# Seventeen gate/up pairs of an FFN by Strassen's algorithm, and the sample states moved from the FFN's input to its output stage

## The chip, the cores and the metric

The kernel runs on one core of a Trainium2 chip. The metric is the device time of one execution in microseconds (us). The kernel before took 1107.72 us (median of three runs, 1106.37 to 1108.14).

## The reference

One step of a decoder layer for a prompt of 512 tokens and 8 sample rows, 520 columns in all, with a model width of 1024, all in float32. What the change touches is the end of the layer and one output of its middle:

```
h2 = rmsnorm(x, norm2_w) * (1 + sc2) + sh2
gt, up = jnp.split(h2 @ w_ffn_in, 2, axis=-1)              # 1024 -> 2 x 2816
x = x + g2 * ((jax.nn.silu(gt) * up) @ w_ffn_out)          # 2816 -> 1024
y = rmsnorm(x, final_norm_w)
...
h_last = h0 * decay + B (outer) (x * dt)                   # SSD state of each sample row, ssm_sample
```

The state of each sample row (32 heads x 64 x 128) is read, scaled, increased by an outer product and written out. Nothing else in the layer's end needs it.

## The kernel before, in words

**Number format.** Every matrix product is made of float32 operands that are cut into a high part (ScalarE casts to fp32r) and a low part (VectorE subtracts the high part from the whole). A product is three matmuls: high x high, high x low, low x high. `parts` (lines 110 to 118) cuts a weight block of 128 x 1024, `split` (155 to 157) an activation, `product` (124 to 129) issues the matmuls. All of them stand on line 129 in the profile, all casts of weights on 116, all low parts on 117.

**FFN input stage.** Tokens lie along the free dimension, as two halves of 260. The 22 x 128 gate columns and the 22 x 128 up columns are taken in 22 pairs: `ffn(j)` (L1374) runs `column` for gate block j and for up block j, each 8 blocks of 128 rows x 3 matmuls x 2 halves, so 96 matmuls of 260 columns to a pair. `ffn_end` (L1348) takes silu of the gate on ScalarE (L1354), multiplies it with the up product on VectorE (L1355), and splits the result into `ah` and `al` (L156, L157).

**FFN output stage.** `ffn_out(j)` (L1410) runs one column of 22 blocks x 3 x 2 = 132 matmuls against `ah` and `al`, for j = 0 to 5; its weights come in three pieces of 8, 8 and 6 blocks. VectorE adds the gated product to the residual (`gate_add`), ScalarE squares it (L390), VectorE sums the squares into `acc`. `last_pair` (L1449) runs the last two columns in two token parts and the last norm with them: TensorE sums `acc` over the partitions (L330) in the middle of the second part.

**Sample states.** 32 units, one or two after each pair of the input stage (`sample_state`, L1334). GpSimd makes three elementwise operations for each (L1342 to L1344), and its queue issues the loads of the state (L1330) and of a B row (L1331), and the write (L1345). State loads run two units ahead over three buffers.

**What sets the order.** The program is a list of steps (`todo`); `perform` runs through it and asks `ahead` to load and cut the weights of the next `LOOK` = 2 units before a step is written down. Weight loads go through SP's queue into `raw` tiles, of which there are `NRAW` = 3. TensorE always runs in the order of the program text. The other engines are ordered by a scheduler with priorities. Each engine takes its instructions in order, and an instruction that waits holds those behind it.

Of the kernel before, what the change touches and what calls it, by code (L numbers as in the profile page):

```python
# [16 lines left out]
P = 128  # L17
T = 520
# [34 lines left out]
def tile_decoder(ctx: ExitStack, tc: tile.TileContext, I: dict, O: dict):  # L53
# [129 lines left out]
    def perform():  # L183
        queue = W["queue"] = [u for us, _ in plan for u in us]
        made = W["made"]
        at = 0
        for us, fn in plan:
            ahead(at + len(us) + (LOOK if at else 0), W["loads"] if made else 0)
# [1035 lines left out]
    def out_open():  # L1224
        for n in ("gt_", "gh_", "tb_"):
            closed(G[n])
        closed(G["ab_"])
        closed(G["yp_"])
        G["fp_"], fp = opened("fp")
        x1 = G["x1"] = fp.tile([P, KD, T], F32, name="x1")  # L1230
        G["RB"] = fp.tile([P, T], F32, name="RB3")
# [7 lines left out]
        G["wo_"], G["wo"] = opened("wo")  # L1239
        a2 = mod[:, U_SC2 : U_SC2 + 8]  # L1240
# [68 lines left out]
    def ffn_act():  # L1309
        closed(G["wo_"])  # L1310
        closed(G["mp_"])
        G["hs_"], G["hs"] = opened("hs")
        G["fq_"], fq = opened("fq", "right")
        G["ah"] = fq.tile([P, NF, T], F32R, name="ah")
        G["al"] = fq.tile([P, NF, T], F32R, name="al")

# [6 lines left out]
    def state_load(n):  # L1323
# [9 lines left out]

    def sample_state(n):  # L1334

        g, b = state_unit(n)
        for i in range(0 if n else 2):
            state_load(i)
        h, bb = states.pop(n)
        at = lambda v: v[:, 2 * g : 2 * g + 2, b : b + 2].rearrange("p j b -> p b j").unsqueeze(3).broadcast_to([P, 2, 2, P])  # L1340
        t = G["hs"].tile([P, 2, 2, P], F32, tag="ht", name=f"ht{n}")
        nc.gpsimd.tensor_tensor(t, bb.unsqueeze(2).broadcast_to([P, 2, 2, P]), at(xds), ALU.mult)  # L1342
        nc.gpsimd.tensor_tensor(h, h, at(dtx[:, 1]), ALU.mult)
        nc.gpsimd.tensor_tensor(h, h, t, ALU.add)  # L1344
        nc.gpsimd.dma_start(out=O["ssms"][g, :, b : b + 2], in_=h)  # L1345
        state_load(n + 2)

    def ffn_end(j, pg, pu):  # L1348

        s = G["ff"].tile([P, T], F32, tag="fs", name=f"fs{j}", bufs=NFS)  # L1350
        with urgent():
            for (g, t0, t1), (u, _, _) in zip(pg, pu):
                view = halves if t1 - t0 == T else lambda ap: ap
                nc.scalar.activation(view(s[:, t0:t1]), g, AF.Silu, bias=0.0, scale=1.0)  # L1354
                nc.vector.tensor_tensor(view(s[:, t0:t1]), u, view(s[:, t0:t1]), ALU.mult)  # L1355
        split(G["ah"][:, j], G["al"][:, j], s)

# [50 lines left out]
    ah, al = (lambda k: G["ah"][:, k]), (lambda k: G["al"][:, k])

    def ffn_out(j):  # L1410
        def fn(*ws):
            ps = column(ws, ah, al)
            x = G["x1"][:, j]
# [35 lines left out]
    def last_pair(*ws):  # L1449
# [139 lines left out]
```

## Time and profile before

| | |
|---|---|
| time, median of 3 runs | 1107.72 us |
| the profiled execution | 1108.36 us |
| its span (first to last instruction) | 1106.6 us |
| TensorE, VectorE, ScalarE, GpSimd busy | 1076.7, 695.7, 463.9, 345.5 us |
| first multiply of pair 0, last of pair 21 (L1355) | 721.1 and 963.8 us |
| first matmul of the output stage | 963.5 us |
| last matmuls of the last pair (L129) | about 1092 us |

Times inside the execution count from the start of its span. A row of a group reads: line, engine, operation, what it writes <- what it reads, shapes, how often; then busy us, mean ns of one; then the engine's idle time just before them and what ended it. A row of a timeline reads: start, duration, engine, line, operation. In a row of windows, behind the stretch and its length, stand busy us and count of TensorE, its weight loads, VectorE, ScalarE and GpSimd, then TensorE's granted clock, the share of the DMA engines and GB/s. A row of a DMA view ends in KB of one transfer and the median us from its issue to its landing; a row of one line or tile gives the shortest, median and longest duration in ns. A row of waits reads: who waited <- for what, us in total, times, longest.

### The profile page before, as it was taken

The page shows a single profiled execution, that of the slowest core. Times are in us where ns is not written, and L with a number is a line of the kernel's source. Part 1 is how long each engine was busy: PE and PEld are TensorE (multiplying, and loading weights), DVE is VectorE, ACT ScalarE, POOL GpSimd, SP SyncE. Part 2 cuts the span into 40 slices and gives each one's busy share as a digit, 9 for nine tenths or more (in the row PEclk, how much of TensorE's full clock was granted, in tenths as well). Part 3 has the DMA queues.
Part 4 walks back from the last instruction along what each step waited for, and adds up shares of the span by engine and source line. Part 5 has one row for each costly group of instructions (what it writes and reads, how often), then busy time and mean ns, then how long its engine had stood idle before and what let it go on. Part 6 is the DMA issues. An engine that isn't in the chain of part 4 may idle for free.

```text
span 1106.6 us, 22150 instructions
## 1 busy us (share of the span) xinstructions
PE 1076.7 (97%) x9331; PEld 1047.9 (95%) x9331; DVE 695.7 (63%) x963; ACT 463.9 (42%) x774; POOL 345.5 (31%) x498
## 2 busy tenths in 40 slices
PE   8988999999999999999999999999999999999995
PEld 6987999999999999999999999799999999999995
DVE  5696787877877698688677655556555543323332
ACT  4448464664664534755433333632222222222220
POOL 1133344243333442000000000489999950000001
PEclk8999999999999999999999999999999999999998
DMA  9435453534624423454434445277666642232212
GB/s 360 193 88 173 144 151 122 191 108 132 191 97 135 170 94 126 135 171 153 153 134 159 147 169 189 91 226 218 202 217 197 208 154 96 86 91 88 86 53 78
DMA packets 58467, 165.34 MB, mean 149 GB/s; under 512 B 10880, under 2 KB 16512, under 8 KB 57600
## 3 DMA queue, kind: packets, MB, share of 16 engines
q1 hardware_dynamic: 51712, 142.96, 39.5%
q0 software_dynamic: 6656, 20.98, 6.3%
q8 instruction: 73, 1.20, 0.4%
q14 instruction: 26, 0.21, 0.1%
HBM read 151.05 MB, written 12.86 MB: 148 GB/s over the span
## 4 chain that ended last, share of the span: by engine, by line
PE 86%; DVE 4%; DMA 3%; ACT 2%; issue 2%; POOL 1%; SPq 0%; DVEq 0%; ACTq 0%; POOLq 0%
PE m L129 75%; PE b L129 4%; DMA raw<-in_win 2%; PE b L795 1%; PE b L207 1%; PE b L770 1%; PE b L797 1%; PE b L301 1%; DVE v L652 1%; PE b L748 1%; POOL hst L775 0%; PE b L731 0%; DVE acc L391 0%; DVE wlo L117 0%; DMA araw<-in_wada 0%
## 5 line engine op out<-in xcount | busy, mean ns | idle before, releaser
L129 PE MATMUL m<-hh,whi 128*128 128x260 f32 (+1 forms) x1840 | 380.8, 287 | 4.5 <-ACT v L644 3.4
L129 PE MATMUL m<-hl,whi 128*128 128x260 f32 (+1 forms) x1840 | 374.4, 284 | 1.1 <-DVE hl L481 1.0
L129 PE MATMUL m<-hh,wlo 128*128 128x260 f32 (+1 forms) x1840 | 374.4, 284 | 0.1
L117 DVE TENSOR_TENSOR wlo<-raw,whi 128x1024 fp32r<-128x1024 f32 (+2 forms) x169 | 231.6, 1373 | 162.6 <-ACT whi L116 159.5
L116 ACT CAST whi<-raw 128x1024 fp32r<-128x1024 f32 (+2 forms) x169 | 173.1, 1027 | 356.2 <-PE m L129 240.5
L129 PEld LDWEIGHTS m<-hh,whi 128*128 128x128 f32 x1840 | 286.0, 189 | 10.4 <-ACT v L644 3.6
L129 PEld LDWEIGHTS m<-hl,whi 128*128 128x128 f32 x1840 | 285.5, 189 | 2.0 <-DVE hl L481 1.6
L129 PEld LDWEIGHTS m<-hh,wlo 128*128 128x128 f32 x1840 | 286.0, 189 | 0.3 <-DVE wlo L117 0.3
L341 POOL TENSOR_TENSOR r<-me,mhalf 128x5 f32<-128x5 f32 (+2 forms) x6 | 6.4, 1064 | 438.2 <-DVE me L340 438.2
L652 DVE SCALAR_TENSOR_TENSOR v<-xb,cwh,v 128x512 f32<-128x512 f32 x96 | 72.1, 752 | 39.9 <-POOL xb L639 19.1
L129 PE MATMUL m<-ah,whi 128*128 128x260 f32 x264 | 53.2, 283 | 0.0
L129 PE MATMUL m<-ah,wlo 128*128 128x260 f32 x264 | 53.1, 282 | 0.0
L129 PE MATMUL m<-al,whi 128*128 128x260 f32 x264 | 53.0, 282 | 0.0
L129 PE MATMUL m<-gh,whi 128*128 128x260 f32 x256 | 52.8, 288 | 0.0
L643 ACT COPY xb<-m 128x520 f32<-128x520 f32 (+1 forms) x31 | 17.9, 577 | 82.2 <-PE m L129 82.2
L1355 DVE TENSOR_TENSOR fs<-m,fs 128x520 f32<-128x520 f32 (+2 forms) x23 | 15.5, 676 | 57.4 <-PE m L129 56.6
L129 PE MATMUL m<-gl,whi 128*128 128x260 f32 x256 | 51.3, 282 | 0.0
L129 PE MATMUL m<-gh,wlo 128*128 128x260 f32 x256 | 51.3, 282 | 0.0
L816 POOL TENSOR_TENSOR h<-h,cc 128x1024 f32<-128x1024 f32 x16 | 39.1, 2444 | 27.4 <-DMA cc<-dbc 26.4
L1342 POOL TENSOR_TENSOR ht<-bb,xds 128x512 f32<-128x512 f32 x32 | 45.3, 1415 | 2.4 <-DMA bb<-dbc 1.9
L1344 POOL TENSOR_TENSOR hs<-hs,ht 128x512 f32<-128x512 f32 x32 | 45.2, 1411 | 0.8
L129 PEld LDWEIGHTS m<-gh,whi 128*128 128x128 f32 x256 | 39.2, 188 | 2.6 <-PE b L301 1.3
(300 smaller groups left out, 1742.6 us busy)
## 6 DMA issues: line engine op xcount, KB each, us to landing
raw<-in_win SPq DMA_DIRECT2D x73, 512.0 KB, 4.9
raw<-in_wfi SPq DMA_DIRECT2D x44, 512.0 KB, 4.4
araw<-in_wada SPq DMA_DIRECT2D x24, 512.0 KB, 3.9
h<-in_sssm SPq DMA_DIRECT2D x16, 512.0 KB, 4.0
raw<-in_wssd SPq DMA_DIRECT2D x16, 512.0 KB, 3.4
hs<-in_sssm POOLq DMA_DIRECT2D x32, 256.0 KB, 4.1
out_ssms<-hs POOLq DMA_DIRECT2D x32, 256.0 KB, 3.3
raw<-in_wfo SPq DMA_DIRECT2D x16, 512.0 KB, 3.5
```

What stands on the lines that cost most here:

```text
L116: nc.scalar.copy(hi, raw)
L117: nc.vector.tensor_tensor(lo, raw, hi.bitcast(F32), ALU.subtract)
L129: nc.tensor.matmul(o, a[:, k, c0 : c0 + P], b[:, t0:t1], start=f, stop=e)
L207: nc.tensor.matmul(ps[32 * i : 32 * i + 32, 0:n], sc[:, k], raw[:, n * i : n * i + n], start=first, stop=last)
L301: nc.tensor.matmul(ps[32 * i : 32 * i + 32, 0:256], scr[:, k], w[:, 256 * i : 256 * i + 256], start=k == 0 and j == 0, stop=k == KD - 1 an ...
L643: nc.scalar.copy(shape(xb[:, 3 + t0 : 3 + t1]), o)
L652: nc.vector.scalar_tensor_tensor(v[:, 0:TP], xb[:, k : k + TP], w(k), v[:, 0:TP], ALU.mult, ALU.add)
L748: nc.tensor.matmul(cb[:, cs], bt[:, cs], ct[:, cs], start=True, stop=True)
L816: nc.gpsimd.tensor_tensor(h0, h0, cc.unsqueeze(2).broadcast_to([P, 4, 2, P]), ALU.mult)
L1342: nc.gpsimd.tensor_tensor(t, bb.unsqueeze(2).broadcast_to([P, 2, 2, P]), at(xds), ALU.mult)
L1344: nc.gpsimd.tensor_tensor(h, h, t, ALU.add)
L1355: nc.vector.tensor_tensor(view(s[:, t0:t1]), u, view(s[:, t0:t1]), ALU.mult)
```

## The change

**Seven products for eight.** Pairs 3 to 19 (`WINO = 3, 20`) are computed by the Winograd form of Strassen's algorithm. The gate block and the up block of a pair are taken as a 2 x 2 block matrix (upper and lower half of the 1024 rows by gate and up), the activations as another (upper and lower half of the rows by the two token halves). `wino` runs seven products of 4 blocks x 3 matmuls, each into a single PSUM bank, in the order g0, g1, y0, x1, y1, z0, x0, and VectorE adds them up out of PSUM. `sums_of_rows` makes the four sums of activation blocks once, behind pair 1, on VectorE and GpSimd, and splits them into `tt`. For each pair `wino_weights` cuts the gate block (cut g) and the lower half of the up block (cut x0), then `wino_sums` makes four sums of weight blocks on GpSimd, in place in the raw tiles, and cuts them: x1 from the first sum, y0 from the third, z from the fourth, y1 from the second. All of it for pair j + 1 is written down while pair j runs. The raw tiles stay three.

**The order of the engines.** From `ffn_act` to the end of the output stage all five engines run in the order of the program text instead of the scheduler's.

**Splitting later.** `ffn_end` no longer splits. The 22 results stay in `as` tiles; ten are split before each of the pairs 20 and 21 and two at the end (`out_rows`, `out_row`), when the space of the Strassen tiles is free.

**States later.** The 32 state units become a generator that is stepped five times in each of the six output columns, and to its end before the last pair. One of the three GpSimd operations becomes four ScalarE activations of 128 x 128, one becomes a VectorE addition, one stays. Each step adds and writes the state of the step before. State tiles have four buffers instead of three.

```diff
+WINO = 3, 20
...
     def ffn_act():
...
-        G["hs_"], G["hs"] = opened("hs")
+        G["ffn"] = tc.manual_schedule(engines={E.PE, E.Activation, E.DVE, E.Pool, E.SP})
+        G["ffn"].__enter__()
+        W["loads"] = 0
...
     def state_load(n):
...
-        h = sp.tile([P, 2, 2, P], F32, tag="hs", name=f"hs{n}", bufs=3)
+        h = sp.tile([P, 2, 2, P], F32, tag="hs", name=f"hs{n}", bufs=4)
         bb = sp.tile([P, 2, P], F32, tag="bb", name=f"bb{n}", bufs=3)
...
+    def sample_states():
+        for n in range(2):
+            state_load(n)
+        before = None
+        for n in range(33):
+            if n < 32:
+                g, b = state_unit(n)
+                state_load(n + 2)
+                h, bb = states.pop(n)
+                at = dtx[:, 1, 2 * g : 2 * g + 2, b : b + 2].rearrange("p j b -> p b j")
+                nc.gpsimd.tensor_tensor(h, h, at.unsqueeze(3).broadcast_to([P, 2, 2, P]), ALU.mult)
...
+                        nc.scalar.activation(t[:, i, j], bb[:, i], AF.Identity, bias=0.0, scale=x)
+            if before:
+                pg, pb_, ph, pt = before
+                nc.vector.tensor_tensor(ph, ph, pt, ALU.add)
+                nc.gpsimd.dma_start(out=O["ssms"][pg, :, pb_ : pb_ + 2], in_=ph)
+            before = (g, b, h, t)
+            yield True
...
     def ffn_end(j, pg, pu):
...
-        split(G["ah"][:, j], G["al"][:, j], s)
...
+    def sums_of_rows():
...
+        for k in range(4):
...
+            p(t3, b[0][1][1], b[0][0][1], minus)
+            p(t3, t3, b[1][1][1], add)
+            p(t3, t3, b[1][0][1], minus)
+            v(t1, b[0][0][1], b[0][0][0], minus)
...
+            v(t4, t4, b[1][1][0], add)
+            for i, t in enumerate((t1, t2, t4, t3)):
+                split(*(x[:, k] for x in G["tt"][(0, 1, 3, 2)[i]]), t)
...
+    def wino_load(j):
+        if WINO[0] <= j < WINO[1]:
+            WW["raw", j] = load(I["wfi"][j]), load(I["wfi"][NF + j])
...
+    def wino_weights(j):
...
+        nc.scalar.copy(hi, g)
+        nc.vector.tensor_tensor(lo, g, hi.bitcast(F32), ALU.subtract)
+        wino_tiles(j, "x")
+        split(*(t[:, 0:4] for t in WW["x", j]), u[:, 4:8])
...
+    def wino_sums(j, between=lambda: None, silu=lambda: None):
...
+        a11, a12, a21, a22 = g[:, 0:4], g[:, 4:8], u[:, 0:4], u[:, 4:8]
...
+        v = nc.gpsimd.tensor_tensor
+        v(a22, a21, a22, ALU.add)
+        v(a21, a11, a21, ALU.subtract)
+        v(a11, a22, a11, ALU.subtract)
+        v(a12, a12, a11, ALU.subtract)
+        cuts = [("x", 1, a22), ("y", 0, a11), ("z", 0, a12), ("y", 1, a21)]
...
+        for hi, lo, a in cuts[:2]:
+            nc.scalar.copy(hi, a)
+        silu()
+        for hi, lo, a in cuts[:2]:
+            nc.vector.tensor_tensor(lo, a, hi.bitcast(F32), ALU.subtract)
+        between()
+        for hi, lo, a in cuts[2:]:
+            split(hi, lo, a)
+        wino_load(j + 1)
...
+    def wino(j):
...
+            nc.scalar.copy(u2, mult("g", 0, B(0, 0)))
+            add(sa, mult("g", 1, B(1, 0)), u2)
+            wino_weights(j + 1)
+            add(u2, mult("y", 0, tt[1]), u2)
+            add(u4, mult("x", 1, tt[0]), u2)
+            o = mult("y", 1, tt[2])
+            add(vb, o, u4)
+            add(va, o, u2)
+            add(sb, mult("z", 0, B(1, 1)), u4)
+            o = mult("x", 0, tt[3])
+            def silu():
+                nc.scalar.activation(s, s, AF.Silu, bias=0.0, scale=1.0)
+            def between():
+                add(va, o, va)
+                nc.vector.tensor_tensor(s, f2, s, ALU.mult)
+            wino_sums(j + 1, between, silu)
...
     def ffn_out(j):
         def fn(*ws):
-            ps = column(ws, ah, al)
+            ps = column(ws, ah, al, lambda kk: states_step() if kk in (4, 8, 12, 16, 20) else None)
```

**VectorE during one pair of the input stage.** Before, pair 10: `fs10` is the multiply, `wlo` the low part of a weight block, `al` the low part of the result.

```order
L1355 TENSOR_TENSOR fs10_10287<-m577_10238,fs10_10287 128x520
L117 TENSOR_TENSOR wlo579_10313<-raw578_10310,whi579_10312 128x1024
L157 TENSOR_TENSOR al_8963<-fs10_10287,ah_8962 128x520
L117 TENSOR_TENSOR wlo581_10319<-raw580_10316,whi581_10318 128x1024
L1355 TENSOR_TENSOR fs11_10420<-m583_10371,fs11_10420 128x520
```

Now, from the second product of pair 7 on: `wglo8`, `wxxlo8`, `wyylo8`, `wzlo8` are low parts of the cuts g, x, y, z of pair 8; `raw564` holds its gate block, `raw565` its up block; `b...` are PSUM banks of pair 7's products, `fs7_0`, `fs7_1` and `as7` its sums.

```order
L1496 TENSOR_TENSOR wglo8_9935<-raw564_9900,wghi8_9934 128x1024
L158 TENSOR_TENSOR wxxlo8_9939<-raw565_9902,wxxhi8_9938 128x512
L1545 TENSOR_TENSOR fs7_0_9904<-b568_9942,fs7_0_9904 128x260
L1545 TENSOR_TENSOR fs7_0_9904<-b569_9956,fs7_0_9904 128x260
L1545 TENSOR_TENSOR fs7_1_9905<-b570_9970,fs7_0_9904 128x260 x2
L1545 TENSOR_TENSOR as7_8982<-b571_9985,fs7_0_9904 128x260
L1521 TENSOR_TENSOR wxxlo8_9939<-raw565_9902,wxxhi8_9938 128x512
L1521 TENSOR_TENSOR wyylo8_10013<-raw564_9900,wyyhi8_10012 128x512
L1545 TENSOR_TENSOR fs7_1_9905<-b572_9999,fs7_1_9905 128x260
L1562 TENSOR_TENSOR as7_8982<-fs7_1_9905,as7_8982 128x520
L158 TENSOR_TENSOR wzlo8_10015<-raw564_9900,wzhi8_10014 128x512
L158 TENSOR_TENSOR wyylo8_10013<-raw565_9902,wyyhi8_10012 128x512
```

The two whole-block subtractions and the two results of a pair became one whole block and five half blocks, and seven adds out of PSUM stand among them. The last reader of `raw564` is the low part of z, last but one in the row; the load of pair 9's up block goes into that tile.

**GpSimd around one sample state.** Before, in the input stage: `hs` are state tiles, `bb` B rows, `ht` the outer product.

```order
L1342 TENSOR_TENSOR ht5_9654<-bb5_9527,xds_94 128x512
L1343 TENSOR_TENSOR hs5_9526<-hs5_9526,dtx_93 128x512
L1331 DMA bb7_9660<-dbc_97 128x256
L1344 TENSOR_TENSOR hs5_9526<-hs5_9526,ht5_9654 128x512
L1343 TENSOR_TENSOR hs6_9650<-hs6_9650,dtx_93 128x512
L1345 DMA out_ssms<-hs5_9526 128x512
L1330 DMA hs7_9659<-in_sssm 128x512
```

Now, in the output stage:

```order
L1363 DMA out_ssms<-hs4_12032 128x512
L1337 DMA hs8_12214<-in_sssm 128x512
L1338 DMA bb8_12215<-dbc_97 128x256
L1353 TENSOR_TENSOR hs6_12104<-hs6_12104,dtx_93 128x512
L1363 DMA out_ssms<-hs5_12068 128x512
L1337 DMA hs9_12250<-in_sssm 128x512
```

Two of the three GpSimd operations left its queue. The load of state 7 went into the tile of state 4 (three buffers); the load of state 8 now goes into the tile of state 4 (four buffers), whose write stands just ahead of it in the queue.

More of the change, by code (lines that the diff above doesn't have):

```diff
@@ L187, in perform @@
         for us, fn in plan:
-            ahead(at + len(us) + (LOOK if at else 0), W["loads"] if made else 0)
+            ahead(at + len(us) + (W["look"] if at else 0), W["loads"] if made else 0)
             got = [made[at + i] for i in range(len(us))]
@@ L1332, in state_load @@
         states[n] = h, bb
[L1334 to L1346, printed above, removed]
@@ new lines, in states_step, with __init__, tile @@
+    def states_step():
+        if "states" not in G:
+            G["states"] = sample_states()
+        return next(G["states"], False)
+    class Scratch:
+        def __init__(self):
+            self.at = {"hi": 0, "lo": 0}
+        def tile(self, shape, dtype, tag=None, name=None, bufs=1):
+            kind = tag.split("_")[0]
+            rows = G["hl" if kind == "lo" else "hh"].rearrange("p a b -> p (a b)")
+            if kind == "sq":
+                return G["ff"].tile([P, T], F32, tag="fs", name=name, bufs=NFS)
+            a = self.at[kind]
+            n = shape[1] * shape[2]
+            self.at[kind] += n
+            return rows[:, a : a + n].rearrange("p (k c) -> p k c", c=shape[2])
@@ L1358, in ffn_first, with out_row, out_rows, fn @@
+    def out_row(k):
+        s, hi = G["as"][k], G["ah"][k]
+        lo = G["fq"].tile([P, T], F32R, tag="as", name=f"al{k}", bufs=NF + 1)
+        G["al"].append(lo)
+        split(hi, lo, s)
+    def out_rows(a, b):
+        def fn():
+            for k in range(a, b):
+                out_row(k)
+        return fn
     def ffn_first(part):
@@ new lines, in wino_sums @@
+    def wino_sums(j, between=lambda: None, silu=lambda: None):
+        if not WINO[0] <= j < WINO[1]:
+            silu()
+            between()
+            return
+        g, u = WW.pop(("raw", j))
+        a11, a12, a21, a22 = g[:, 0:4], g[:, 4:8], u[:, 0:4], u[:, 4:8]
+        wino_tiles(j, "y")
+        wino_tiles(j, "z")
+        v = nc.gpsimd.tensor_tensor
[4 more added lines that the diff above has]
+        cuts = [("x", 1, a22), ("y", 0, a11), ("z", 0, a12), ("y", 1, a21)]
+        cuts = [(*(t[:, 4 * h : 4 * h + 4] for t in WW[n, j]), a) for n, h, a in cuts]
+        for hi, lo, a in cuts[:2]:
+            nc.scalar.copy(hi, a)
+        silu()
+        for hi, lo, a in cuts[:2]:
+            nc.vector.tensor_tensor(lo, a, hi.bitcast(F32), ALU.subtract)
+        between()
+        for hi, lo, a in cuts[2:]:
+            split(hi, lo, a)
+        wino_load(j + 1)
@@ new lines, in wino, with fn, mult @@
+    def wino(j):
+        def fn():
+            f1, f2 = (G["ff"].tile([P, T], F32, tag="fs", name=f"fs{j}_{i}", bufs=NFS) for i in range(2))
+            u2, u4, va, vb = f1[:, 0:H2], f1[:, H2:T], f2[:, 0:H2], f2[:, H2:T]
+            s = G["as"][j]
+            sa, sb = s[:, 0:H2], s[:, H2:T]
+            tt = G["tt"]
+            B = lambda r, c: (hblock("hh", r, c), hblock("hl", r, c))
+            def mult(kind, half, x):
+                hi, lo = WW[kind, j]
+                o = bank()[:, 0:H2]
+                for k in range(4):
+                    q = 4 * half + k
+                    for a, b, f, e in ((hi, x[0], k == 0, False), (hi, x[1], False, False), (lo, x[0], False, k == 3)):
+                        nc.tensor.matmul(o, a[:, q], b[:, k], start=f, stop=e)
+                return o
+            add = lambda out, a, b: nc.vector.tensor_tensor(out, a, b, ALU.add)
+            nc.scalar.copy(u2, mult("g", 0, B(0, 0)))
+            add(sa, mult("g", 1, B(1, 0)), u2)
+            wino_weights(j + 1)
+            add(u2, mult("y", 0, tt[1]), u2)
[11 more added lines that the diff above has]
+            wino_sums(j + 1, between, silu)
+            for kind in "gxyz":
+                WW.pop((kind, j))
```

101 lines of the change are left out of this document (82 added, 19 removed).

## The prediction

> **What bounds the kernel now.** I read the page first, then the stretches by window, then the timeline of the FFN input stage.
>
> ```profile
> span 1106.6 us, 22150 instructions
> PE 1076.7 (97%) x9331; PEld 1047.9 (95%) x9331; DVE 695.7 (63%) x963; ACT 463.9 (42%) x774; POOL 345.5 (31%) x498
> PE 86%; DVE 4%; DMA 3%; ACT 2%; issue 2%; POOL 1%; SPq 0%; DVEq 0%; ACTq 0%; POOLq 0%
> ```
>
> TensorE is busy for 97% of the span and makes 86% of the chain that ended last. The windows say whether that is so in the two stages that change:
>
> ```profile
> 850.00:900.00 50.00, 50.00 (x419) 50.00 (x418) 28.12 (x18) 12.70 (x16) 49.05 (x49) 1.00 0.62 194
> 950.00:1000.00 50.00, 50.00 (x419) 50.00 (x418) 15.51 (x22) 13.24 (x16) 0.00 (x0) 1.00 0.31 94
> ```
>
> In both, 419 matmuls in 50 us at a granted clock of 1.00: 119.3 ns each, no gap. In the first, GpSimd is full too (49.05 of 50, the sample states); VectorE and ScalarE have room. The timeline of VectorE gives the period of one gate/up pair:
>
> ```profile
> 929.19 0.70 DVE L1355 TENSOR_TENSOR fs<-m,fs 128x520 f32<-128x520 f32 x1 [3.72 <-PE m L129]
> 930.02 1.23 DVE L117 TENSOR_TENSOR wlo<-raw,whi 128x1024 fp32r<-128x1024 f32 x1
> 931.16 0.69 DVE L157 TENSOR_TENSOR al<-fs,ah 128x520 fp32r<-128x520 f32 x1
> 940.73 0.70 DVE L1355 TENSOR_TENSOR fs<-m,fs 128x520 f32<-128x520 f32 x1 [3.72 <-PE m L129]
> ```
>
> 940.73 - 929.19 = 11.54 us for 96 matmuls. So TensorE bounds the stage, and only what stays below its pace is free.
>
> **What the products save.** A Strassen pair has 7 products of 4 x 3 matmuls: 84 for 96, each still 260 wide, so 84 x 119.3 = 10.02 us. That is 1.43 us for each of 17 pairs, 24.3 us, if TensorE keeps the pace.
>
> **The loop around a Strassen pair.** What must run in turn, once per pair, is priced from the quiet part of the stage:
>
> ```profile
> L117 DVE TENSOR_TENSOR wlo<-raw,whi 128x1024 fp32r<-128x1024 f32 x10 | 12.2, 1225 | 20.3 <-ACT whi L116 19.6
> L116 ACT CAST whi<-raw 128x1024 fp32r<-128x1024 f32 x10 | 10.5, 1054 | 41.8 <-issue 21.1 <-PE m L129 20.7
> L1355 DVE TENSOR_TENSOR fs<-m,fs 128x520 f32<-128x520 f32 x5 | 3.5, 700 | 18.6 <-PE m L129 18.6
> L157 DVE TENSOR_TENSOR al<-fs,ah 128x520 fp32r<-128x520 f32 x5 | 3.5, 694 | 0.0
> L156 ACT CAST ah<-fs 128x520 fp32r<-128x520 f32 x5 | 3.1, 627 | 0.0
> raw<-in_wfi SPq DMA_DIRECT2D x5, 512.0 KB, 3.5
> 925.50 0.33 SPq L107 DMA_DIRECT2D raw<-in_wfi  x1
> 924.25 1.23 DVE L117 TENSOR_TENSOR wlo<-raw,whi 128x1024 fp32r<-128x1024 f32 x1 [3.93 <-ACT whi L116]
> L1344 POOL TENSOR_TENSOR hs<-hs,ht x32: 1290/1308/2159, 725.2 to 897.6; 128x512 f32<-128x512 f32 x32
> ```
>
> A weight load is issued 0.02 us after VectorE releases its buffer (924.25 + 1.23 = 925.48, then 925.50) and lands 3.5 us later. A 512-wide piece costs a little under the 520-wide rows: 0.62 on ScalarE, 0.68 on VectorE. A GpSimd sum of two 128x512 tiles takes 1.30.
>
> There are three raw buffers and each pair takes two, so the up weights of pair n+1 land in the buffer that held the gate weights of pair n. Their load waits for the last reader there, VectorE's low part of cut z. And z is the fourth of four GpSimd sums in a row, each reading the one before; the first overwrites half of the up weights, so it waits for the load and for cut x0. Hence a ring: load 3.5, cast x0 0.62, low x0 0.68, four sums 5.2, cast z 0.62, low z 0.68, an estimated 0.3 for the handovers (one of them is the 0.02 above): **11.6 us at the least**, longer than TensorE's 10.02 and than the 11.54 of today.
>
> Two things lengthen it. First, VectorE takes its work in order: low y0, the add of product 7 (0.43, by the 0.424 of a 256-wide multiply in the last row below), the multiply of 0.69, then low z. Second, GpSimd and VectorE hinder each other:
>
> ```profile
> 803.88 1.41 POOL L1342 TENSOR_TENSOR ht<-bb,xds 128x512 f32<-128x512 f32 x1
> 804.29 1.55 DVE L157 TENSOR_TENSOR al<-fs,ah 128x520 fp32r<-128x520 f32 x1
> 805.25 1.50 POOL L1343 TENSOR_TENSOR hs<-hs,dtx 128x512 f32<-128x512 f32 x1
> L1343 POOL TENSOR_TENSOR hs<-hs,dtx x32: 1047/1072/2025, 722.6 to 896.5; 128x512 f32<-128x512 f32 x32
> L1355 DVE TENSOR_TENSOR fs<-m,fs x23: 424/700/700, 721.1 to 963.8; 128x520 f32<-128x520 f32 x21, 128x256 f32<-128x256 f32 x1, 128x264 f32<-128x264 f32 x1
> ```
>
> The 0.69 us subtraction lasts 1.55 beside GpSimd: it gets going when L1342 ends at about 805.3, and L1343 (1.07 by median) lasts 1.50 as it waits for the subtraction in turn. The multiply out of PSUM never takes more than 0.70, beside GpSimd or not. In the ring: from the release, landing at 3.5, x0 low at 4.9, two sums at 7.5; low x1 squeezes in, so the third sum ends at 9.35 and the fourth at 10.65; low y0, blocked until then, ends at 11.3; add 11.75, multiply 12.45, low z **13.1**. I take 13.1: it is the case without slack, but every row of it is measured. Ends: 11.6, and 14.1 with the load at 4.5, the median in the busy stretch (row below). The four single PSUM banks add nothing: product 7 waits for the bank of product 3, whose add stands behind low x0, and that wait lies inside the 3 us that TensorE idles anyway.
>
> The Trainium skill says of this port (SBUF — State Buffer, "SBUF: two separate sides") that GpSimd and a VectorE instruction with two SBUF inputs lock each other out for a whole instruction. The rows above agree. Without the lock the ring would be 12.1 and the sum below 16 us smaller.
>
> **The sums of rows, before pair 3.** 44 VectorE instructions 260 wide and 12 on GpSimd stand behind pair 1's multiply; pair 3's cuts stand behind them.
>
> ```profile
> 732.92 0.70 DVE L1355 TENSOR_TENSOR fs<-m,fs 128x520 f32<-128x520 f32 x1 [2.75 <-PE m L129]
> L157 DVE TENSOR_TENSOR hl<-xn,hh 128x256 fp32r<-128x256 f32 x8 | 3.1, 422 | 2.0 <-ACT hh L156 2.0
> L1440 POOL TENSOR_TENSOR x<-x,RB 128x256 f32<-128x256 f32 x2 | 1.4, 736 | 5.5 <-ACT RB L1436 5.5
> ```
>
> 44 x 0.427 = 18.8 us; with GpSimd's 12 x 0.74 locked out, 27.7. I take 24, as GpSimd starts early. From 733.6 that is 757.6; pair 2 hides only 11.5 of it. Then low g, low x0, three sums with low x1 between, the rest of the fourth, low y0: 766.1 for the start of pair 3's third product; low z 766.8. Sixteen rings: 976.4; pair 19's y0 stands 1.8 before, 974.6. Five products (7.16), the add, the multiply and pair 20's first low part (2.35 and 0.2, less the 0.5 that needs only high parts): pair 20 starts at 983.8. Before, it starts two pairs ahead of the output stage:
>
> ```profile
> L129 PE MATMUL m<-ah,whi x264: 278/283/286, 963.5 to 1058.0; 128*128 128x260 f32 x132
> 1078.23 0.50 PE L330 MATMUL b<-cst,acc 128*128 128x1 f32 x4
> ```
>
> 963.5 - 23.1 = 940.4. **Term 1: +43.4 us** (19 with a ring of 11.6, 59 with 14.1; 4 either way for the sums). At TensorE's own pace of 10.02 it is -5.9. The row splits in pairs 20 and 21 cost nothing: ten of 0.69 and two weight parts of 1.23 are 9.4 of VectorE's 11.5 us. The norm row moved to another pool adds no instruction.
>
> **The states in the output stage.** Taking them out of the input stage gains nothing by itself: TensorE had no gap there. Per state and in GpSimd's order: state load, B load, multiply, write of the state before.
>
> ```profile
> raw<-in_wfi SPq DMA_DIRECT2D x31, 512.0 KB, 4.5
> out_ssms<-hs POOLq DMA_DIRECT2D x31, 256.0 KB, 3.2
> out_ssms<-hs POOLq DMA_DIRECT2D x1, 256.0 KB, 2.5
> out_ssms<-hs POOLq DMA_DIRECT2D x1, 256.0 KB, 4.9
> L1331 POOL DMA_DIRECT2D bb<-dbc x32 | 18.7, 585 | 0.0
> L1345 POOL DMA_DIRECT2D out_ssms<-hs x32 | 18.2, 568 | 0.6 <-POOL hs L1344 0.6
> L1330 POOL DMA_DIRECT2D hs<-in_sssm x32 | 18.0, 561 | 1.4 <-DMA out_ssms<-hs 0.9 <-issue 0.6
> POOL hs L1330 <- DMA out_ssms<-hs: 0.9, 1, 0.9
> ```
>
> With four buffers, load n+2 takes the buffer of state n-2, and that one is written out as the last thing of the step before. So GpSimd issues a write and then stands at the next load until it has landed. Before, the load waited for an older write: 0.9 us in the whole stage. One step is now 3.2 + 0.56 + 0.59 + 1.07 + 0.1 = **5.5 us**; 4.8 with the quickest write shown, 7.2 with the slowest; five steps, 27.5, for a column of 132 matmuls, 15.85.
>
> This reaches TensorE because ScalarE and VectorE take a column's states ahead of the gate add and of the next column's third weight block. The first write goes out about 15 us after the output stage starts (16 of 22 blocks, 11.45, then cast, products, add). The statistics of the last pair stand behind the add of state 30, which follows write 28 by 0.57 + 1.07 + 0.69, then two adds of 0.43: 15 + 28 x 5.5 + 3.4 = 172.4. Today they run at 1078.2 - 963.5 = 114.7. **Term 2: +57.7 us** (38 at 4.8; 77 at 6.2, midway up). ScalarE's four small products per state, each under the 0.627 of a 520-wide cast, stay inside the step.
>
> The Trainium skill (TensorE: Matmul & The Clock Gate, "HAM oscillation") has the clock halved after a gap of about 3.4 us. The granted clock was 1.00 in the windows above, which have no gap. By that rule the last stall costs 1.7 us more and the sum is 1211.
>
> **Sum.** The profiled execution took 1108.36 us, 0.64 above the median of 1107.72. 1108.36 + 43.4 + 57.7 - 0.64 = **1209 us**.
>
> **Rivals.** (a) The products set the pace after all, and the states hide: 1107.7 - 5.9 = 1102, faster. It decides if the ring is below 10.4 us (43.4 - 16 x 2.7 = 0) and the step below 3.5 (15 + 28 x 3.5 + 3.4 is about today's 114.7). VectorE's room speaks for it; a 3.5 us load ahead of 5.2 us of sums against it. (b) Only the ring binds, the writes land before GpSimd asks: 1151. For it: they hardly ever delayed GpSimd before. Against: the order. (c) Only the states bind, cuts keep up: 1107.7 - 5.9 + 57.7 = 1160. (d) Writes land at 4.9 among loads and a step takes 7.2: 1107.7 + 43.4 + 105 = 1256.
>
> **Chances.** Forecast 0.70; (a) 0.05, (b) 0.10, (c) 0.08, (d) 0.07. The forecast's own ends, 1163 and 1244, do not all come together. With (b) the range 1150 to 1245 leaves out (a) and (d), 0.12. Runs agree within 0.2%, so a difference under that is none: faster 0.04, same 0.01 (both out of (a)), slower 0.95.
>
> **What would show it.** Right: 13 us from one Strassen pair to the next, ScalarE's x0 cast waiting for the load, TensorE for low y0; TensorE idle for about 12 us before pair 3; GpSimd waiting some 100 us for its writes; columns 27 us apart. Wrong, if TensorE stays gapless between pairs 4 and 19, or if the output columns stay 16 us apart.

## The result, and the profile after

The changed kernel takes 1213.66 us (median of four runs, 1212.39 to 1215.2), the kernel before 1107.05 beside it (1105.97 to 1108.14): a ratio of 1.0964, 95% interval 1.0945 to 1.0983. The forecast was 1209, in a range of 1150 to 1245.

The page of the changed kernel, its first two lines and the chain of work that ended last by engine and by line:

```profile
span 1211.3 us, 22506 instructions
PE 1083.4 (89%) x9127; PEld 1041.0 (86%) x9127; DVE 793.2 (65%) x1226; ACT 543.5 (45%) x1003; POOL 355.2 (29%) x514
PE 54%; DMA 15%; POOL 12%; DVE 7%; issue 6%; ACT 5%; SPq 0%; POOLq 0%; DVEq 0%; ACTq 0%
PE m L130 45%; DMA out_ssms<-hs 7%; DMA raw<-in_wfi 5%; POOL hs L1353 2%; POOL raw L1513 2%; PE b L130 2%; DMA araw<-in_wad 2%; POOL raw L1512 2%; POOL raw L1511 2%; PE b L796 1%; POOL hs L1337 1%; PE b L771 1%; POOL bb L1338 1%; PE b L798 1%; DVE wxxlo L158 1%
```

TensorE issues 204 matmuls less and is busy a little longer (1083.4 us for 1076.7), but its share of the chain fell from 86% to 54%. What came in has names: the states' writes (`out_ssms<-hs`, 7%), the FFN input weights' loads (`raw<-in_wfi`, 5%), and the GpSimd sums of weight blocks, L1511 to L1513. None of these stood among the lines that the page of the kernel before lists for its chain.

The windows, one row from the Strassen pairs and one from the output columns:

```profile
780.00:830.00 50.00, 41.42 (x320) 38.92 (x319) 34.07 (x56) 18.87 (x32) 21.95 (x16) 1.00 0.19 68
1060.00:1090.00 30.00, 18.87 (x132) 18.36 (x132) 9.78 (x14) 11.30 (x28) 13.56 (x21) 0.78 0.52 158
```

Where 419 matmuls stood in 50 us, there are now 320; in the output stage 132 in 30 us, one column. No engine is full in either: the fullest is TensorE, with 41.42 of 50 us and 18.87 of 30.

**The Strassen pairs.** One row of the GpSimd sum L1511, which comes once a pair, gives their period, 208.1 / 16 = 13.0 us. Then one turn of the ring, from the timelines of VectorE, SP's queue and ScalarE, and the waits of 770 to 980:

```profile
L1511 POOL TENSOR_TENSOR raw<-raw x17: 1277/1282/1293, 755.6 to 963.7; 128x512 f32<-128x512 f32 x17
...
851.58 1.22 DVE L1521 TENSOR_TENSOR wyylo<-raw,wyyhi 128x512 fp32r<-128x512 f32 x1 [1.83 <-ACT wyyhi L1518]
...
853.86 0.68 DVE L158 TENSOR_TENSOR wzlo<-raw,wzhi 128x512 fp32r<-128x512 f32 x1
...
854.58 0.93 SPq L108 DMA_DIRECT2D raw<-in_wfi  x2
...
858.06 0.62 ACT L157 CAST wxxhi<-raw 128x512 fp32r<-128x512 f32 x1 [3.41 <-DMA raw<-in_wfi]
...
ACT wxxhi L157 <- DMA raw<-in_wfi: 51.5, 15, 3.5
PE b L1542 <- DVE fs L1545: 17.4, 15, 1.2
PE b L1542 <- DVE wyylo L1521: 12.0, 16, 0.8
```

Low z ends at 854.54, the up load is issued 0.04 us later, ScalarE gets its data at 858.06 after 3.41 us of standing still, fifteen times in the window. TensorE stands twice a pair, for an add and for low y0. The add is that of product 3, whose bank product 7 takes; both stands lie beside the ring and not in it, since in this window the adds on VectorE waited for TensorE only four times, 2.5 us in all.

**Ahead of pair 3.** The timelines of VectorE and TensorE:

```profile
737.76 0.86 DVE L1466 TENSOR_TENSOR ft<-ft,hl 128x260 f32<-128x260 f32 x1
...
752.94 0.42 DVE L158 TENSOR_TENSOR t2l<-ft,t2h 128x260 fp32r<-128x260 f32 x1
...
753.75 0.59 PE L1542 MATMUL b<-hh,wghi 128*128 128x260 f32 x1 [9.88 <-ACT wghi L1495]
...
761.90 0.39 PE L1542 MATMUL b<-t1h,wyylo 128*128 128x260 f32 x1 [0.74 <-DVE wyylo L1521]
```

The sums of rows end on VectorE at 753.36. The cast of g for pair 3 stands on ScalarE behind the casts of these sums, and TensorE has waited 9.88 us when it starts on it at 753.75; the first product with low y0 starts at 761.90.

**The output stage.** Its first column, the states' writes and the statistics, with one step on GpSimd between, and the waits from 985 to the end:

```profile
L130 PE MATMUL m<-ah,whi x264: 277/283/588, 1002.4 to 1153.8; 128*128 128x260 f32 x132
L1363 POOL DMA_DIRECT2D out_ssms<-hs x32: 539/585/588, 1018.0 to 1181.0; - x32
...
1084.65 0.54 POOL L1337 DMA_DIRECT2D hs<-in_sssm  x1 [3.79 <-DMA out_ssms<-hs]
1085.18 0.54 POOL L1338 DMA_DIRECT2D bb<-dbc  x1
1085.73 1.06 POOL L1353 TENSOR_TENSOR hs<-hs,dtx 128x512 f32<-128x512 f32 x1
1086.72 0.58 POOL L1363 DMA_DIRECT2D out_ssms<-hs  x1
1089.63 0.54 POOL L1337 DMA_DIRECT2D hs<-in_sssm  x1 [2.33 <-DMA out_ssms<-hs]
...
POOL hs L1337 <- DMA out_ssms<-hs: 82.8, 28, 5.1
PE m L130 <- ACT whi L117: 39.3, 5, 9.5
...
1175.30 0.58 POOL L1363 DMA_DIRECT2D out_ssms<-hs  x1
...
1180.20 1.01 PE L331 MATMUL b<-cst,acc 128*128 128x1 f32 x4 [5.95 <-DVE acc L392]
```

In brackets behind each load stands what GpSimd waited for: the write that it had issued just before. 28 such waits make 82.8 us. TensorE pays once a column, in the end: five waits, 39.3 us, for weight casts that stand on ScalarE behind the column's states and its squares.

From these rows the whole difference of the spans, 1211.3 - 1106.6 = 104.7, splits into three: the output stage starts 38.9 later (1002.4 for 963.5), it takes 63.1 more up to the statistics (177.8 for 114.7), and the end takes 2.7 more (31.1 for 28.4). Of the 63.1, TensorE's waits are 48.7 (39.3 and 3.5 for weight parts, 5.9 for the statistics); the other 14.4 stand beside a lower granted clock, 0.78 in the row above, and were not separated further.

### The profile page after: what moved, and what is told of

Its sections match the earlier page's. It is cut to its first block, busy times and chain, and to the rows that moved or that the text cites. A ratio compares the mean times of both kernels' runs of the same rounds, so it can differ in the third digit from the quotient of the medians.

```text
span 1211.3 us, 22506 instructions
## 1 busy us (share of the span) xinstructions
PE 1083.4 (89%) x9127; PEld 1041.0 (86%) x9127; DVE 793.2 (65%) x1226; ACT 543.5 (45%) x1003; POOL 355.2 (29%) x514
## 4 chain that ended last, share of the span: by engine, by line
PE 54%; DMA 15%; POOL 12%; DVE 7%; issue 6%; ACT 5%; SPq 0%; POOLq 0%; DVEq 0%; ACTq 0%
PE m L130 45%; DMA out_ssms<-hs 7%; DMA raw<-in_wfi 5%; POOL hs L1353 2%; POOL raw L1513 2%; PE b L130 2%; DMA araw<-in_wad 2%; POOL raw L1512 2%; POOL raw L1511 2%; PE b L796 1%; POOL hs L1337 1%; PE b L771 1%; POOL bb L1338 1%; PE b L798 1%; DVE wxxlo L158 1%
## 5 line engine op out<-in xcount | busy, mean ns | idle before, releaser
L130 PE MATMUL m<-hh,whi 128*128 128x260 f32 (+1 forms) x1296 | 271.9, 289 | 4.7 <-ACT v L645 3.4
L130 PE MATMUL m<-hh,wlo 128*128 128x260 f32 (+1 forms) x1296 | 265.1, 284 | 1.1 <-DVE wlo L118 1.0
L130 PE MATMUL m<-hl,whi 128*128 128x260 f32 (+1 forms) x1296 | 265.1, 284 | 0.6 <-DVE hl L158 0.2
L130 PEld LDWEIGHTS m<-hh,whi 128*128 128x128 f32 x1296 | 202.5, 190 | 11.0 <-ACT v L645 3.6
L118 DVE TENSOR_TENSOR wlo<-raw,whi 128x1024 fp32r<-128x1024 f32 (+1 forms) x132 | 163.6, 1249 | 70.3 <-ACT whi L117 69.7
L130 PEld LDWEIGHTS m<-hh,wlo 128*128 128x128 f32 x1296 | 202.4, 190 | 1.5 <-DVE wlo L118 1.5
L130 PEld LDWEIGHTS m<-hl,whi 128*128 128x128 f32 x1296 | 202.2, 190 | 1.3 <-DVE hl L158 0.8
L117 ACT CAST whi<-raw 128x1024 fp32r<-128x1024 f32 (+1 forms) x132 | 133.2, 1020 | 137.0 <-PE m L130 107.8
L130 PE MATMUL m<-ah,whi 128*128 128x260 f32 x264 | 58.3, 305 | 39.3 <-ACT whi L117 39.3
L130 PEld LDWEIGHTS m<-ah,whi 128*128 128x128 f32 x264 | 45.4, 210 | 40.3 <-ACT whi L117 40.3
L1511 POOL TENSOR_TENSOR raw<-raw 128x512 f32<-128x512 f32 x17 | 21.8, 1285 | 126.4 <-DVE wxxlo L158 126.4
L130 PEld LDWEIGHTS m<-ah,wlo 128*128 128x128 f32 x264 | 45.1, 209 | 4.9 <-DVE wlo L118 4.9
```

The lines of the kernel that those rows point to most:

```text
L117: nc.scalar.copy(hi, raw)
L118: nc.vector.tensor_tensor(lo, raw, hi.bitcast(F32), ALU.subtract)
L130: nc.tensor.matmul(o, a[:, k, c0 : c0 + P], b[:, t0:t1], start=f, stop=e)
L1511: v(a22, a21, a22, ALU.add)
```

## The experiments

The theory was the prediction's: a ring through the three raw buffers sets the pairs, a ring through the four state buffers sets the output stage. Each kernel below changes one thing in the changed kernel unless it says otherwise, and none leaves out work. Ratios are to the kernel before, run beside them (1107 to 1108). "Pair" is the period of the GpSimd sum, "write" the mean from one state write to the next, "stage" the time from the first matmul of the output stage to the first statistics.

| kernel | us | ratio, 95% interval | pair | write | stage |
|---|---|---|---|---|---|
| changed | 1213.66 | 1.0964 (1.0945 to 1.0983) | 13.01 | 5.26 | 177.8 |
| z_first | 1200.88 | 1.0842 (1.0808 to 1.0876) | 12.21 | 5.24 | |
| four_raws | 1178.04 | 1.0632 (1.0601 to 1.0664) | 10.78 | 5.20 | |
| x0_first, with four_raws | 1169.59 | 1.0566 (1.0551 to 1.0582) | 10.16 | 5.26 | |
| spread | 1204.81 | 1.0884 (1.0865 to 1.0903) | 13.01 | 5.28 | |
| five_states | 1169.74 | 1.0549 (1.0509 to 1.0589) | 12.99 | 3.83 | 135.5 |
| near_load | 1174.03 | 1.0596 (1.0566 to 1.0627) | 13.03 | 3.89 | 136.7 |
| states_only | 1175.49 | 1.0616 (1.0598 to 1.0634) | | 5.29 | 178.6 |
| all_mended | 1107.30 | 1.0010 (0.9986 to 1.0034) | 10.17 | 3.79 | 127.8 |
| late_states | 1104.13 | 0.9962 (0.9945 to 0.9978) | 10.17 | 3.75 | 120.2 |

**A shorter ring: z_first.**

```diff
-        between()
-        for hi, lo, a in cuts[2:]:
-            split(hi, lo, a)
+        split(*cuts[2])
+        between()
+        split(*cuts[3])
```

> Edit: VectorE takes low z ahead of the add of product 7 and the multiply, instead of behind them. No instruction is added or taken away. Theory (the ring goes from low z through the up load): the ring is shorter by that add and multiply, 0.42 + 0.70 = 1.1 us, so a pair takes 11.9 us and 16 x 1.1 = 18 us go: about 1196 (1192 to 1200). Rival (the order in VectorE does not matter, since VectorE's or GpSimd's whole work sets the pair): the time stays at 1210 to 1215.

Measured 1200.88, a pair every 12.21 us (L1511 of this kernel):

```profile
L1511 POOL TENSOR_TENSOR raw<-raw x17: 1273/1284/1295, 755.6 to 951.0; 128x512 f32<-128x512 f32 x17
```

Nothing was taken from VectorE or GpSimd, and 12.8 us went, so it is the place in the ring that counts. It is 0.8 a pair and not 1.1. Low z starts 1.36 us behind the start of low y0, where it was 2.28 in the changed kernel (851.58 to 853.86): 0.92 less, since low z now has to wait for its own cast, which the add and the multiply used to cover. The other tenth is not in this part of the ring. The rows of ScalarE and VectorE:

```profile
871.29 0.62 ACT L157 CAST wzhi<-raw 128x512 fp32r<-128x512 f32 x1 [0.21 <-POOL raw L1514]
...
870.58 1.23 DVE L1521 TENSOR_TENSOR wyylo<-raw,wyyhi 128x512 fp32r<-128x512 f32 x1 [1.83 <-ACT wyyhi L1518]
871.94 0.69 DVE L158 TENSOR_TENSOR wzlo<-raw,wzhi 128x512 fp32r<-128x512 f32 x1
```

Low y0 ends at 871.81, the cast at 871.91, and low z starts behind the later of the two.

**The ring cut: four_raws.** The low parts of g and z keep one buffer each (that part of the edit isn't shown), and the third one becomes a home for the up weights of every second pair.

```diff
+            g, src = load(I["wfi"][j]), I["wfi"][NF + j]
+            if (j - WINO[0]) % 2 == 0:
+                WW["raw", j] = g, load(src)
+            else:
+                if "spare" not in WW:
+                    WW["spare"] = wp.tile([P, KD, P], F32R, tag="lo", name="spare")
+                u = WW["spare"].bitcast(F32)
+                nc.sync.dma_start(out=u, in_=src)
+                WW["raw", j] = g, u
```

> Edit: the up weights of every second Strassen pair land in a fourth buffer (the low parts of g and z keep one buffer each, which frees one), so a pair's up load waits for a reader two pairs back and not for low z of the pair before. Nothing else is changed. Theory (the ring through the raw buffer sets the pair): L1511 starts about 10.0 us apart (13.0 now), because TensorE's 84 products of 119.3 ns come last; 16 x 3.0 = 48 us go, 1213.7 becomes about 1166 (1160 to 1175). Rival (VectorE and GpSimd, which get no less to do, set the pair): the pairs stay 13 us apart and the time stays at 1205 to 1214. Between the two, if the four sums one behind the other still come last: 11 to 12 us, 1180 to 1198.

Measured 1178.04: 35.6 us went, which neither VectorE nor GpSimd could have given, but a pair takes 10.78 us, not 10.0. The theory's direction holds; its next bound was wrong, and the time is 3 us above the expected range. What is late now, in the timelines of GpSimd (L1523 to L1526, the sums) and VectorE:

```profile
863.28 1.29 POOL L1523 TENSOR_TENSOR raw<-raw 128x512 f32<-128x512 f32 x1 [5.04 <-DVE wxxlo L158]
...
866.02 1.62 POOL L1525 TENSOR_TENSOR raw<-raw,raw 128x512 f32<-128x512 f32 x1
867.72 1.30 POOL L1526 TENSOR_TENSOR raw<-raw 128x512 f32<-128x512 f32 x1
...
868.33 1.24 DVE L1533 TENSOR_TENSOR wyylo<-raw,wyyhi 128x512 fp32r<-128x512 f32 x1 [1.83 <-ACT wyyhi L1530]
...
872.17 1.22 DVE L1508 TENSOR_TENSOR wglo<-raw,wghi 128x1024 fp32r<-128x1024 f32 x1
```

No load is in it. GpSimd waits 5.04 us for low x0, makes its four sums, and only when the fourth ends at 869.02 does low y0 get through; then VectorE runs an unbroken row of eight up to the next low x0. The two take turns.

**The turns shortened: x0_first.** On top of four_raws; `wino_weights` is parted into x0 (0) and g (1).

```diff
+            wino_weights(j + 1, 0)
             nc.scalar.copy(u2, mult("g", 0, B(0, 0)))
             add(sa, mult("g", 1, B(1, 0)), u2)
-            wino_weights(j + 1)
+            wino_weights(j + 1, 1)
```

> Edit, on top of the four raw buffers (1178.0, a pair every 10.78 us): the high and low parts of x0 of the next pair are made ahead of the add of product 2 and of g's parts, instead of behind them. No instruction is added or taken away. Theory (with the load out of the ring, GpSimd and VectorE take turns: GpSimd's four sums 5.74 us from low x0 to the end of the fourth, then VectorE's low y0, add, multiply, low z, low y1, add of product 2, low g, low x0, 5.04, together 10.78): without the add and low g between, 1.47 us go, the turn is 9.3, TensorE's 10.02 comes last, and 16 x 0.76 = 12 us go: about 1166 (1163 to 1170). Rival (the 10.8 us are TensorE's products with their gaps, or VectorE's whole work): 1176 to 1180.

Measured 1169.59, a pair every 10.16 us, and TensorE has no gap any more (the window of 50 us, and below it the second sum in this kernel):

```profile
780.00:830.00 50.00, 50.00 (x415) 49.94 (x414) 47.47 (x69) 23.34 (x40) 31.03 (x20) 1.00 0.29 106
...
L1524 POOL TENSOR_TENSOR spare<-raw,spare x8: 2152/2156/2162, 767.4 to 909.8; 128x512 f32<-128x512 f32 x8
```

The theory holds, with a gain of 8.5 for the 12 expected: at 415 matmuls in 50 us the 84 of a pair take 10.12 us, not 10.02, and 16 x (10.78 - 10.16) is 9.9. VectorE does the same work in 10.16 us as in 13.0, so its amount never was the bound. What I had not foreseen is the second row: low g now runs beside the second sum, which grows from 1.29 to 2.16 us.

**The sums of rows: spread.**

```diff
     todo(ffn_first(1))
+    todo(lambda: sums_of_rows((0, 1)))
...
         if j == 1:
-            todo(sums_of_rows)
+            todo(lambda: sums_of_rows((2, 3)))
```

> Edit, on the changed kernel as it is: two of the four groups of sums of rows are made behind pair 0 and two behind pair 1, instead of all four behind pair 1. The same instructions. Theory (pair 3 waits for VectorE, which is in the sums until 753): the 9.9 us for which TensorE waits for g of pair 3, and some of what follows, go: about 1203 (1200 to 1206). Rival (pair 3 waits for its own cuts and GpSimd sums, which take as long wherever the sums of rows stand): 1210 to 1215.

Measured 1204.81, 8.9 us less. Pair 3's first sum starts at 746.7 instead of 755.6, so all of it comes from there; of TensorE's waits ahead of the pair's third product there remain 0.76 us for low g and these, for cuts of its own weights (timeline of TensorE):

```profile
751.77 0.39 PE L1542 MATMUL b<-t1h,wyyhi 128*128 128x260 f32 x1 [2.79 <-ACT wyyhi L1518]
753.02 0.39 PE L1542 MATMUL b<-t1h,wyylo 128*128 128x260 f32 x1 [0.74 <-DVE wyylo L1521]
```

**The states' ring, cut in two ways: five_states and near_load.** The first takes a fifth buffer, the second loads one step ahead instead of two with the four there are. In both the load meets a write that was issued one step earlier.

```diff
+        if n % 5 < 4:
             h = sp.tile([P, 2, 2, P], F32, tag="hs", name=f"hs{n}", bufs=4)
+        else:
+            if n == 4:
+                G["spare"] = G["fq"].tile([P, T], F32, tag="as", name="spare", bufs=NF + 1)
+            h = G["spare"][:, 0 : 4 * P].rearrange("p (a b c) -> p a b c", a=2, b=2)
```

```diff
-        for n in range(2):
+        for n in range(1):
...
-                state_load(n + 2)
+                state_load(n + 1)
```

> Edit: a fifth state buffer (in a row that is free by then), so the load of state n+2 takes the buffer of state n-3, whose write was issued a whole step earlier, instead of n-2, whose write was issued just ahead. Nothing else is changed. Theory (the wait for the write's landing sets the step): a step falls from 5.26 us to 3.2 to 3.6, the columns come near TensorE's 15.85, and 28 x 1.8 = 50 us go: about 1163 (1155 to 1175). Rival (the transfers themselves, 0.64 MB a step besides the weights, set the step, whoever waits): the step stays near 5 us and the time above 1200.

> Edit: with the four buffers as they are, a state is loaded one step ahead instead of two, so the load takes the buffer of state n-3 as well. No buffer is added; the load has less time to land. Theory (the wait for the write's landing sets the step): the step is then set by GpSimd's own 2.7 us or by the load's landing, 3.3; about 3.4 us a step, 1213.7 - 28 x 1.86 = 1162 (1155 to 1175), the same as with a fifth buffer. Rival (transfers set the step): above 1200, or slower than now, since the loads start later.

Measured 1169.74 and 1174.03: 43.9 and 39.6 us went. The transfers did not grow shorter, they were only no longer waited for. The median landing of a state write is 3.4 and 3.2 us here, for 2.8 in the changed kernel. The waits of 1000 to 1180, first with the fifth buffer, then with the near load, and below these one row of VectorE's timeline with the near load:

```profile
POOL out_ssms L1368 <- DVE spare L1367: 19.8, 6, 4.0
...
POOL spare L1342 <- DMA out_ssms<-spare: 10.8, 5, 2.7
```

```profile
POOL out_ssms L1363 <- DVE hs L1362: 53.7, 7, 32.2
...
POOL hs L1337 <- DMA out_ssms<-hs: 13.4, 6, 3.1
...
1050.47 3.31 DVE L118 TENSOR_TENSOR wlo<-raw,whi 128x768 fp32r<-128x768 f32 x3 [0.78 <-ACT whi L117]
```

GpSimd's wait for its writes fell from 82.8 us to 13.4 with the near load, TensorE's for the casts from 39.3 to 10.1 and 9.0. (Of the 53.7 us, 32.2 are one wait at the start, ahead of the first write.) Both versions do the same, with a buffer more and without one, so it is the distance between a write and the load that reuses its buffer that decides. The six columns still take 19 us each on the mean, not 16: a step takes 3.8 us, and now GpSimd waits for VectorE's adds, which stand behind weight parts (the last row: 3.31 us of them ahead of two adds).

**One part alone: states_only.**

```diff
-WINO = 3, 20
+WINO = 3, 3
...
-        if j == 1:
-            todo(sums_of_rows)
```

(The row splits stay ahead of pairs 20 and 21, and the weights are loaded as before.)

> Edit: one part of the change alone. No pair is made by Strassen's algorithm and no sums of rows are made; the states stand in the output stage with four buffers, as in the changed kernel. Theory (the two terms add up, and the states' is set by the write's landing): before plus the states' term as the changed kernel has it, 177.8 us from the start of the output stage to the last statistics against 114.7, so about 1107 + 63 = 1170 (1160 to 1174). Rival (the states are late only because the Strassen pairs hand them a late start or a full VectorE): 1105 to 1130.

Measured 1175.49: 68.1 more than before, with pairs that are the old ones (and 1.5 above the expected range). The wait and TensorE's share of it are those of the changed kernel (waits of 960 to 1173):

```profile
POOL hs L1337 <- DMA out_ssms<-hs: 83.2, 28, 5.6
...
PE m L130 <- ACT whi L117: 40.3, 5, 11.3
```

So the states' term does not depend on Strassen's algorithm; the other 38.5 of the 106.6 come with the pairs. This kernel also keeps the fixed order of the engines and the later splitting; its output stage starts at 962.9, for 963.5 before, so neither costs anything ahead of it.

**All mends together, and the states spread further: all_mended and late_states.** The first takes four_raws, x0_first, five_states and spread, and queues the next column's weight parts between the states' steps (first diff); the second also moves eight states into the last pair (second diff, its lower part in `last_pair`).

```diff
+    todo(set_ahead(0, 2))
...
+            n = len(W["made"])
+
+            def between(kk):
+                if kk in (4, 8, 12, 16, 20):
+                    states_step()
+                if kk in (8, 16):
+                    ahead(n + kk // 8, 1)
```

```diff
-                if kk in (4, 8, 12, 16, 20):
+                if kk in (5, 10, 15, 20):
...
+                        if kk in (7, 14, 21) and part + i < 2:
+                            states_step()
```

> Edit: the four raw buffers, x0 first, the fifth state buffer and the spread sums of rows together; and in the output stage the weight parts of the next column are queued at blocks 8 and 16 of a column, between the states' steps, instead of ahead of all five of them. Theory (each of these waits costs what it measured alone, and nothing else binds): 1213.7 - 36 - 12 - 44 - 10 = 1112, and the columns, 19.0 us apart with the fifth buffer alone, come to 16 to 17.5 when ScalarE and VectorE no longer take a column's states in one go: 12 to 18 less, about 1097 (1090 to 1112). That would be 1% below before, of the 24.3 us that the products can save. Rival (the saved products are lost to the transfers of the states, 0.64 MB a step beside 1.4 MB of weights a column): columns stay at 19 and the time at 1110 to 1125, no better than before.

> Edit, on top of all the mends together (1107.3, the same as before): four states in each of the six columns and eight in the last pair, instead of five in each column and the rest ahead of the last pair's weights. Theory (there a state still takes 3.8 us from write to write, so five do not fit a column of 15.85 us; they fall behind, and the cast of the last pair's weights and column 5 stand behind them on ScalarE: the last statistics come 127.8 us after the start of the output stage, 114.7 before): four fit, 15.2 for 15.85; the last statistics come 115 to 119 us after the start, and 9 to 13 us go: about 1096 (1093 to 1101), 1% below before. Rival (the last pair, with its weights from two columns, is late for the loads of its weights among the states' transfers, whichever order they have): 1104 to 1110; or the last eight states now hold the end of the kernel: above 1110.

Measured 1107.30, no difference from before that can be told, and 1104.13, a ratio of 0.9962 with an interval that ends below 1: a difference of 0.4%, 3.8 us where I expected 11, outside the expected range. The first four columns of all_mended take 15.8 us each, the fifth some 18: the states have fallen behind, and the last pair's weights wait (1015 to the end, TensorE's longest wait):

```profile
PE b L130 <- ACT whi L117: 4.8, 1, 4.8
```

What the new place of the weight parts is worth by itself was not tried.

In late_states all six columns keep TensorE's pace, and one wait of more than 1.2 us is left (920 to the end):

```profile
PE b L331 <- DVE acc L392: 5.8, 1, 5.8
```

There the square sums stand behind state adds on VectorE. The time lies where the rival had it (1104 to 1110), but the rival's cause, weights of the last pair that load late, is not among TensorE's waits. Of the 24.3 us of the products 13.8 are still there when this kernel's output stage starts (949.7 for 963.5); the output stage gives back 5.5 (120.2 for 114.7) and the end 3.5 (31.9 for 28.4).

## Why the prediction was right, and where its sizes were off

**What TensorE saves.** Right, but only to be had when nothing else binds: 10.16 us a pair in x0_first, for 10.02.

**The ring.** Forecast 13.1, measured 13.0, with the wait at the load and TensorE's wait for low y0 as named. The turn agrees step by step: from the load's issue to the end of low z are 12.98 us (841.56 to 854.54, timelines of SP's queue and VectorE), and the next issue follows at 854.58. The 13.1 rested on GpSimd and VectorE locking each other out. The trace bears that out: L1513, beside low x1, takes 1.62 us where L1511 takes 1.28 (median rows of all 17 each).

```profile
L1513 POOL TENSOR_TENSOR raw<-raw,raw x17: 1597/1620/1623, 758.4 to 966.5; 128x512 f32<-128x512 f32 x17
```

The rule of the Trainium skill (SBUF — State Buffer, "SBUF: two separate sides"), by which one of the two has the shared port for a whole instruction, agrees with this and with the 2.16 us in x0_first, where the instruction on the other side was twice as long.

**The sums of rows.** Forecast 24 us, measured 20: they end at 753.36, counted from the 733.6 of the forecast, nearer to the bound of 18.8 without a lock than to the 27.7 with all of it. Half of GpSimd's twelve were done before 721; beside the other six, six of VectorE's took 0.84 to 0.86 instead of 0.43, like the one at 737.76. Pair 3's third product so starts at 761.9 and not at 766.1, and term 1 is 38.9 instead of 43.4. The mechanism was right; term 1 was too large by a tenth.

**The states.** The step was forecast at 5.5; from the first write at 1018.0 to write 28 at 1175.30 it is 5.62. (The 5.26 in the table holds the last three, which load nothing.) Two parts of it were off and partly made up for each other: from the issue of a write until GpSimd went on are 3.5 us on the mean of the 28 (82.8 / 28 + 0.58), not 3.2, and the rest of the step takes 2.1 and not 2.3. The stage was forecast at 172.4 and takes 177.8: 0.6 from a later first write, 3.3 from 28 steps, 1.5 from what follows write 28 (4.9 for 3.4). Term 2 is 63.1 instead of 57.7.

**The end.** The sum had nothing for it; it takes 2.7 us more. First the second set of statistics, before and after, then a window: the gap ahead of the statistics is 5.95 us, and the granted clock behind it is low:

```profile
L330 PE MATMUL m<-cst,acc x4: 166/250/250, 1087.5 to 1087.8; 128*128 128x1 f32 x4
L331 PE MATMUL m<-cst,acc x4: 164/250/250, 1191.4 to 1191.7; 128*128 128x1 f32 x4
...
1180.00:1190.00 10.00, 9.80 (x66) 9.80 (x67) 3.48 (x12) 0.80 (x2) 2.03 (x4) 0.78 0.15 58
```

Before, the same stretch (1078 to 1088) has no gap and a clock of 1.00. From the first statistics to the second are 11.2 us, for 9.3 before: 2.0 of the 2.7. In all_mended, where TensorE has no gap there, they are 9.3 again (1075.3 to 1084.6), so this part goes with the gap. The other 0.8 lies behind the last statistics, in all_mended too, and its cause is open. The rule of the Trainium skill (TensorE: Matmul & The Clock Gate, "HAM oscillation") that a gap of some 3.4 us halves the clock agrees with the gap of 5.95 us; as a bound it does not hold here, since 2.45 us were enough in near_load (last section). The estimate of 1.7 us that I worked out by it and left out of the sum belonged in it.

**The sum.** That the total came within 5 us is partly luck: the terms were off by -4.5, +5.4 and +2.7. (The lower of the forecast's own ends is 1165 by its own terms, not 1163.) The signs named came: TensorE idle for 12.7 us ahead of pair 3 (9.88, 0.46, 1.57 and 0.74), columns 27 to 29 us apart, and 82.8 us of GpSimd's waits for its writes, where I had said some 100.

**The rivals.** That only the ring or only the states bind (b, c) is out: four_raws and five_states each give back their own part, and states_only has the states' part without any ring. Rival (d) did not come: it had a landing of 4.9 us and a step of 7.2, and measured are 3.5 on the mean and 5.62. (The median of 2.8 misleads here: a sum of steps goes by the mean, and the longest landing is 5.3.) Rival (a), the products set the pace, became true in the pairs with two mends (x0_first), and in the six columns only in late_states.

Two of the later expectations named the wrong next bound. When four_raws took the load out of the ring I took TensorE to be next, and overlooked that low x0 and low y0 hand the work back and forth between two engines that each run in order: 10.78. When five_states took the write's landing out, I took the load's landing or GpSimd's own work to be next, and for the larger part it was the queue on VectorE: 3.8 a step. (z_first was out of its expected range too, by 0.9 us.)

## What to carry to other kernels

When an algorithm takes work from the engine that binds, write down the ring that each buffer closes (last reader, load, first reader, back to the last reader) and compare its length with the new, shorter period, not with the old one. Before a buffer is reused, count how many steps lie between the write out of it and the load into it: one step instead of none was worth 40 us here, and needed no memory. When a ring is cut, look for the next one before counting on the engine's own pace: two engines that run in order and hand work to each other twice per step are a ring too.

## What the runs showed of the hardware that I had not expected

TensorE's clock bore the short gaps of the Strassen pairs: TensorE loses 2.2 us a pair there, in gaps of up to 1.2 us, and the granted clock stays at 1.00 (window of 780 to 830). Behind the gap of 9.88 us ahead of pair 3 it is 0.50, and the matmuls start 0.22 us apart instead of 0.12, until 757.56, 3.8 us later:

```profile
753.70:757.60 3.90, 3.39 (x14) 3.09 (x15) 1.83 (x3) 1.14 (x2) 1.89 (x2) 0.50 0.00 0
...
757.56 0.33 PE L1542 MATMUL b<-hl,wghi 128*128 128x260 f32 x1
```

A gap need not be that long. In near_load TensorE waits 2.45 us ahead of the statistics, and behind it the granted clock is 0.50 for 6.4 us, longer than behind the 9.88:

```profile
1140.65 1.01 PE L331 MATMUL b<-cst,acc 128*128 128x1 f32 x4 [2.45 <-DVE acc L392]
...
1140.60:1147.00 6.40, 6.35 (x29) 6.35 (x30) 0.16 (x1) 0.00 (x0) 0.72 (x1) 0.50 0.11 41
```

In five_states the gap there is 1.40 us, and from 1141 to 1144 the clock is 0.50 as well. What tells these gaps from the harmless 1.2 us of the pairs, no run shows.

The price of a GpSimd and VectorE collision goes by the length of the other's instruction: a GpSimd sum of two 128x512 tiles takes 1.29 us alone, 1.62 beside a 512-wide low part, 2.16 beside a 1024-wide one.
